# A weight ring laid out by rows, and padding that starts every large matmul operand on a multiple of 64 bytes

## The chip, the cores and the metric

The kernel runs on one core of a Trainium2 chip. The metric is the device time of one execution in microseconds, the median of the runs shown. PE is the matrix engine, PEld its weight loads, DVE the vector engine, ACT the scalar engine, POOL the general engine, SP the queue that issues most transfers (DMAs). SBUF is the on-chip memory from which the engines read; an address below is a byte address within one of its 128 partitions. PSUM takes the results of matmuls.

## The reference, cut to what matters

One block of a hybrid transformer with 2048 tokens of width 1024: normalized and modulated input, a projection to 2832 columns, sliding-window attention beside a bidirectional mLSTM scan, an output projection, and 16 experts that each choose 256 tokens.

```python
hx = modulate(rmsnorm(x, norm1_w), sh1, sc1)
hc = modulate(rmsnorm(ctx, norm1_w), csh1, csc1)
aq, ak, av, mq, mk, mv, mo, gates = jnp.split(h @ w_in, offs, -1)     # for hx and for hc
att = latent_attention(apply_rope(aq), apply_rope(ak), av, cak, cav, sink)
h_sum = bidir_mlstm(mq, mk, mv, li_f, lf_f, li_b, lf_b, st_f, st_b)
x = x + g1 * (concat(att, mlstm_out(h_sum, mo, mlstm_norm_w)) @ w_out)
hx2 = modulate(rmsnorm(x, norm2_w), sh2, sc2)
aff = softmax(hx2 @ w_router); gate, idx = top_k(aff.T, 256)          # per expert
y = (silu(xg @ w_gate) * (xg @ w_up)) @ w_down * gate                 # xg = hx2[idx]
x = x + g2 * zeros.at[idx].add(y)
```

## The kernel before

All large products are kept near fp32 accuracy: each fp32 operand is split into a rounded part (hi, type fp32r) and the rest (lo, fp32r), and three matmuls hi·hi, lo·hi, hi·lo are added up in PSUM. A matmul takes a stationary operand (lhsT, 128 columns, loaded by a LDWEIGHTS) and a moving one (rhs, 256 to 512 columns, streamed). For each operand a partition's row is read from one start address on.

The program has three stages that follow each other.

- **The input stage** (48 to 920 us in the trace). Tokens come in units of 256 (`make_hx` writes hx_hi and hx_lo, 8 tiles of 128 rows by 256 tokens). The 2832 columns of w_in are taken in 22 pieces of 128 columns, in an order of groups (kv, q, mk, mq, mv, mo), four times over, once for each pair of units. `weights` (L717) loads a piece in two halves into w_raw, `split_w` (L745) writes w_hi (ACT, L750) and w_lo (DVE, L756) into a ring of four slots; with the group kv come 16 gate columns, 8 with each of its two pieces, by a small DMA of their own (L739). `tok_chain` (L762) makes outputs with tokens on the partitions: stationary hx, moving a pair of slots (L773), 24 matmuls. `chan_chain` (L779) makes outputs with channels on the partitions: stationary one slot, moving hx (L791). Attention runs in between: scores (L257, L261), transposes of the probabilities (L302), products with the values (L330, L331).
- **The mixing stage** (920 to 1445 us): the mLSTM visits (L1907, L1636) with operands of 258 columns (`vsplit`, `split_state`), and the output projection (`proj`, L1998) with 512 moving columns. Then comes the choice of tokens (to about 1525 us).
- **The expert stage** (1525 to 2093 us): per expert 16 transposes of gathered rows (L2589), 192 matmuls for gate and up (`expert`, L2645; stationary ew, moving xg) and 48 with 512 columns for down (`down`, L2697; stationary h, moving ew).

The order of the instructions is made at build time by a small planner (class Flow): tasks wait for tokens (buffers) and events, each step states the engine and a cost, and the planner always takes the step that can start first, by priority. A cost that is changed, or a wait, shifts the order within a stage. Tiles of one pool stand one behind the other in a partition; a tile starts on a multiple of 32 bytes, and pools on the right side are stacked from the top end.

Of the kernel before, what the change touches and what calls it, by code (L numbers as in the profile page):

```python
# [21 lines left out]
F32 = mybir.dt.float32  # L22
F32R = mybir.dt.float32r
# [332 lines left out]
class Kernel:  # L356
# [18 lines left out]
    def constants(self):  # L375
# [18 lines left out]
        nc.vector.tensor_scalar(self.qw, rows[:, 0:64], -(64 ** -0.5), None, op0=OP.mult)  # L394
        self.nsink = const.tile([128, 8], F32, name="nsink")
        nc.vector.tensor_scalar(self.nsink, self.sink, -1.0, None, op0=OP.mult)
        self.identr = const.tile([128, 128], F32R, name="identr")
# [39 lines left out]
    def phase_in(self):  # L437
        nc, tc = self.nc, self.tc
        with ExitStack() as st:
            pool = lambda name, bufs, **k: st.enter_context(tc.tile_pool(name=name, bufs=bufs, **k))  # L440
            self.ps = pool("psin", 1, space=PSUM)
            self.right, self.mod, self.att = ExitStack(), ExitStack(), ExitStack()
            self.keep = self.outer.enter_context(tc.tile_pool(name="gkeep", bufs=1, side="right"))
            self.hxp = self.right.enter_context(tc.tile_pool(name="hxp", bufs=2, side="right"))
            self.hxs = [self.hx_pair(self.hxp, i) for i in range(2)]
            self.early = ExitStack()
            self.ep = self.early.enter_context(tc.tile_pool(name="early", bufs=1, side="right"))
            self.wp = pool("wring", 1)
            self.w_hi = self.wp.tile([128, 4, KT, 136], F32R, name="w_hi")
            self.w_lo = self.wp.tile([128, 4, KT, 136], F32R, name="w_lo")  # L450
            self.mp = self.mod.enter_context(tc.tile_pool(name="mod", bufs=1))
# [116 lines left out]
    def mod_first(self):  # L568
# [66 lines left out]
        self.pin = self.pool("pin", 2, reuse_waits="tile")  # L635
        self.pa = self.att.enter_context(self.tc.tile_pool(name="att", bufs=2, reuse_waits="tile"))
        self.kt = one.tile([128, 2, 2, NSLOT * 128], F32R, name="kt")
        self.ckt = one.tile([128, 2, 2, 2 * 128], F32R, name="ckt")
# [78 lines left out]
    def weights(self):  # L717
        nc, p, fl, tok = self.nc, self.wp, self.fl, self.tok
        n = 0
        for b in range(4):  # L720
            for name, i in GROUPS:
                c0 = {"kv": 512, "q": 0, "mk": 1280, "mq": 768, "mv": 1792, "mo": 2304}[name] + 256 * i
                for j in range(2):
                    yield tok["slot"]
                    sl = n % 4
                    extra = 2816 + 8 * j if name == "kv" else None
                    w = 128 if extra is None else 136
                    left = [2]
                    if n < 4:
                        yield self.wm_ev[XW_AT[2 + n // 2]]  # L730
                    for k0 in range(0, KT, 4):
                        yield tok["w_raw"]
                        raw = self.buf(p, "w_raw", [128, 4, 136])
                        ks = k0 * 128 * W_COLS
                        yield Q(544)
                        nc.sync.dma_start(raw[:, :, :128], self.dram(self.a["w_in"], ks + c0 + 128 * j,
                                                                     [[W_COLS, 128], [128 * W_COLS, 4], [1, 128]]))
                        if extra is not None:
                            nc.sync.dma_start(raw[:, :, 128:], self.dram(self.a["w_in"], ks + extra,  # L739
                                                                         [[W_COLS, 128], [128 * W_COLS, 4], [1, 8]]))  # L740
                        fl.spawn(self.split_w(raw, sl, k0, w, left, n), PRI["wsp"])
                        fl.issued()
                    n += 1

    def split_w(self, raw, sl, k0, n, left, s):  # L745
        nc, fl = self.nc, self.fl
        for k in range(0, 4, 2):
            hi, lo = (w[:, sl, k0 + k:k0 + k + 2, :n] for w in (self.w_hi, self.w_lo))
            yield A(2 * n)
            nc.scalar.activation(hi, raw[:, k:k + 2, :n], AF.Copy)  # L750
            if WPOOL and k:
                yield G(2 * n)
                nc.gpsimd.tensor_sub(lo, raw[:, k:k + 2, :n], f(hi))
            else:
                yield V(2 * n)
                nc.vector.tensor_sub(lo, raw[:, k:k + 2, :n], f(hi))  # L756
        fl.give(self.tok["w_raw"])
        left[0] -= 1
        if not left[0]:
            fl.fire(self.w_ev[s])  # L760

    def tok_chain(self, sl, unit, t, n):  # L762
        hi, lo, _ = self.hx[unit]
# [3 lines left out]
        for hx, w, evs in ((hi, self.w_hi, self.hh_ev), (lo, self.w_hi, self.hl_ev), (hi, self.w_lo, self.hh_ev)):  # L767
            for k in range(KT):
                if k % CH == 0:
                    for ev in evs[unit][k // 2:(k + CH + 1) // 2]:  # L770
                        yield ev
                    yield "P", CH * (0.108 if n == 128 else 0.114)
                self.nc.tensor.matmul(ps[:, :2 * n].rearrange("p (a b) -> p a b", a=2),  # L773
                                      lhsT=hx[:, k, t * 128:(t + 1) * 128], rhs=w[:, sl:sl + 2, k, :n],
                                      start=(i == 0), stop=(i == 23))
# [3 lines left out]
    def chan_chain(self, sl, units):  # L779
        yield self.tok["mm"]  # L780
        ps = self.buf(self.ps, "mm", [128, 512])
        for j, u in enumerate(units):
            hi, lo, _ = self.hx[u]
            i = 0
            for w, hx, evs in ((self.w_hi, hi, self.hh_ev), (self.w_hi, lo, self.hl_ev), (self.w_lo, hi, self.hh_ev)):
                for k in range(KT):
                    if k % CH == 0:
                        for ev in evs[u][k // 2:(k + CH + 1) // 2]:
                            yield ev
                        yield "P", CH * 0.108  # L790
                    self.nc.tensor.matmul(ps[:, j * 256:(j + 1) * 256], lhsT=w[:, sl, k, 0:128], rhs=hx[:, k, :],  # L791
                                          start=(i == 0), stop=(i == 23))
# [3 lines left out]
    def main(self):  # L796
        fl, tok = self.fl, self.tok
        ctx, n = ("c", 0), 0
        for b in range(4):
            xs = [("x", 2 * b), ("x", 2 * b + 1)]  # L800
            for g in GROUPS:
# [16 lines left out]
                else:  # L818
                    for u in units:
                        yield self.hh_ev[u][0]  # L820
                        for t in range(2):
                            ps = yield from self.tok_chain(sl, u, t, 136 if name == "kv" else 128)
                            if name == "kv":
                                fl.spawn(self.when_open(self.kv_out(ps, u, t)), PRI["kv"])
                            elif name == "q":
# [116 lines left out]
    def head_norm(self, ps, nh, used):  # L942
# [11 lines left out]
        nc.scalar.activation(sq, xr, AF.Square)  # L954
        ss = p.tile([128, nh], F32, name=f"hss{nh}", bufs=3)
        yield V(n)
# [68 lines left out]

    def kv_out(self, ps, u, t):
        nc, p, fl, tok = self.nc, self.pin, self.fl, self.tok
# [13 lines left out]
        def value():  # L1041
            if not ctx and n >= NSLOT:
                yield self.unit_done[n - NSLOT + 1]
            vt = (self.cvt if ctx else self.vt)[:, n if ctx else n % NSLOT]
            pv = ps[:, 136:264].rearrange("p (k d) -> p k d", k=2)
            yield A(128)
# [9 lines left out]
        yield V(16)  # L1056
        pg = ps[:, :272].rearrange("p (a b) -> p a b", a=2)[:, :, 128:136]
        nc.vector.tensor_add(g, pg, self.bg.rearrange("p (a b) -> p a b", a=2))
        used()
        xr = yield from self.head_norm(ps[:, :128], 2, used)  # L1060
        if ctx:
# [522 lines left out]
    def split_state(self, d, C):  # L1584
        nc, p = self.nc, self.pin
        cs = p.tile([128, 4, 258], F32R, name=f"cs{d}", bufs=1)
        for j in range(2):
# [95 lines left out]
    def vsplit(self, vr):  # L1683
        nc = self.nc
        vs = self.buf(self.pin, "vsl", [128, 4, 258], F32R)
        yield from self.copy("v_h", 516, vs[:, :, 0:129], vr)
# [810 lines left out]
    def picks(self):  # L2497
# [4 lines left out]
        self.pg = self.pool("pgather", 2)  # L2502
        p16 = self.p16
        oh = [keep.tile([128, 16, 16], F16, name=f"oh0{i}") for i in range(2)]
        for i in range(2):
# [280 lines left out]
```

## Time and profile before

| what | value |
|---|---|
| median of 3 runs | 2085.2 us (2082.46 to 2087.51) |
| the profiled execution's own time | 2095.2 us |
| its span, first to last instruction | 2093.2 us |
| busy PE, PEld, DVE, ACT, POOL | 90%, 80%, 82%, 59%, 41% |
| mean granted clock of PE | 0.95 |
| instructions of PE | 12921 matmuls |

A matmul's busy time in the profile is longer than the step from one matmul to the next, because they overlap in the engine. How long a stream of equal matmuls takes is read from the start times: the start of one group of x8 to the start of the next, divided by 8. The chain of waits does this too: its pieces do not overlap, so a piece "x168" of 19.61 us has a step of 19.61 / 168 us.

### The profile page before, as it was taken

How to read it: one execution, taken by the hardware profiler on the slowest of the kernel's cores; microseconds unless marked ns; L12 is line 12 of the kernel's file. 1: busy time of each engine (PE TensorE's matmuls, PEld its weight loads, DVE VectorE, ACT ScalarE, POOL GpSimd, SP SyncE). 2: the span in 40 equal slices, each digit the busy share in tenths (PEclk: the TensorE clock that was granted, in tenths of full speed). 3: DMA queues.
4: the chain of work that ended last, by engine and by line, in shares of the span. 5: the costliest groups of instructions: out<-in, count | busy, mean ns of one | idle time of the engine just before them, and what ended most of it. 6: DMA issues, size and time to landing. Idle time of an engine off the chain costs nothing.

```text
span 2093.2 us, 37150 instructions
## 1 busy us (share of the span) xinstructions
PE 1881.3 (90%) x12921; PEld 1677.4 (80%) x12921; DVE 1710.0 (82%) x3846; ACT 1226.6 (59%) x2993; POOL 861.1 (41%) x828
## 2 busy tenths in 40 slices
PE   7799999999999999978888798896299999999997
PEld 3688988898889988966666576685299999999996
DVE  3799679999998799869999999976867777777773
ACT  4477667787777777765555355454254545454541
POOL 0224234423442233225777755421343545444432
PEclk9899999999999999988999899898599999999999
DMA  7343264354432332246666565546358787888782
GB/s 275 96 141 100 71 198 112 118 156 133 116 96 77 96 104 76 80 131 216 213 220 197 180 196 175 165 159 209 128 163 256 223 256 222 256 221 259 220 243 41
DMA packets 291195, 345.14 MB, mean 165 GB/s; under 512 B 27032, under 2 KB 225336, under 8 KB 290112
## 3 DMA queue, kind: packets, MB, share of 16 engines
q1 hardware_dynamic: 280768, 307.64, 47.4%
q0 software_dynamic: 9376, 34.08, 7.0%
q8 instruction: 102, 1.67, 0.3%
q10 hardware_dynamic: 864, 1.05, 0.1%
q14 instruction: 85, 0.70, 0.1%
HBM read 266.50 MB, written 76.09 MB: 164 GB/s over the span
## 4 chain that ended last, share of the span: by engine, by line
PE 54%; DVE 28%; issue 6%; DMA 5%; ACT 5%; POOL 1%; SPq 1%; POOLq 0%; DVEq 0%; ACTq 0%
PE gu L2645 17%; PE mm L773 10%; PE yp L2697 8%; PE po L1998 4%; DVE w_lo L756 3%; DMA w_raw<-in_w_in 2%; PE t L302 2%; PE s L257 1%; PE o L608 1%; PE t L2589 1%; DVE s L279 1%; PE o L331 1%; PE o L330 1%; DVE vsl L1615 1%; ACT w_hi L750 1%
## 5 line engine op out<-in xcount | busy, mean ns | idle before, releaser
L2494 ACT ACTIVATE ew_hi<-ew_raw 128x1024 fp32r<-128x1024 f32 x192 | 202.1, 1056 | 157.7 <-PE yp L2697 91.8
L2454 DVE TENSOR_TENSOR ew_lo<-ew_raw,ew_hi 128x1024 fp32r<-128x1024 f32 x152 | 217.4, 1439 | 33.3 <-issue 17.9
L290 POOL TENSOR_SCALAR P<-P,am 128x640 f32<-128x640 f32 (+1 forms) x128 | 115.0, 899 | 261.9 <-DVE am L288 105.3
L756 DVE TENSOR_TENSOR w_lo<-w_raw,w_hi 128x256 fp32r<-128x256 f32 (+1 forms) x352 | 161.6, 484 | 19.0 <-ACT w_hi L750 17.6
L2717 POOL DMA_INDIRECT out_x<-y,idx x32 | 57.6, 1801 | 271.6 <-DVE y L2711 184.9
L773 PE MATMUL mm<-w_hi,hx_hi 128*128 128x256 f32 (+1 forms) x944 | 144.4, 291 | 5.0 <-DVE moe L933 2.0
L2645 PE MATMUL gu<-xg_hi,ew_hi 128*128 128x256 f32 x1024 | 148.9, 283 | 0.0
L750 ACT ACTIVATE w_hi<-w_raw 128x256 fp32r<-128x256 f32 (+1 forms) x352 | 133.9, 409 | 18.4 <-DMA w_raw<-in_w_in 17.2
L773 PE MATMUL mm<-w_hi,hx_lo 128*128 128x256 f32 (+1 forms) x944 | 142.6, 289 | 0.0
L773 PE MATMUL mm<-w_lo,hx_hi 128*128 128x256 f32 (+1 forms) x944 | 142.6, 287 | 0.0
L2645 PE MATMUL gu<-xg_lo,ew_hi 128*128 128x256 f32 x1024 | 141.7, 280 | 0.0
L2645 PE MATMUL gu<-xg_hi,ew_lo 128*128 128x256 f32 x1024 | 141.4, 280 | 0.0
L773 PEld LDWEIGHTS mm<-w_hi,hx_hi 128*128 128x128 f32 x944 | 125.7, 192 | 8.2 <-DVE moe L933 2.6
L2645 PEld LDWEIGHTS gu<-xg_hi,ew_hi 128*128 128x128 f32 x1024 | 131.8, 189 | 0.1
L2645 PEld LDWEIGHTS gu<-xg_lo,ew_hi 128*128 128x128 f32 x1024 | 129.7, 189 | 0.0
L2645 PEld LDWEIGHTS gu<-xg_hi,ew_lo 128*128 128x128 f32 x1024 | 129.3, 188 | 0.0
L773 PEld LDWEIGHTS mm<-w_hi,hx_lo 128*128 128x128 f32 x944 | 126.0, 192 | 2.9 <-issue 2.1
L773 PEld LDWEIGHTS mm<-w_lo,hx_hi 128*128 128x128 f32 x944 | 125.2, 190 | 2.4 <-issue 1.5
L313 DVE TENSOR_TENSOR pl<-t,ph 128x512 fp32r<-128x512 f32 x156 | 105.6, 683 | 23.6 <-ACT ph L311 22.6
L2711 DVE SCALAR_TENSOR_TENSOR y<-yp,gv,g2b 128x512 f32<-128x512 f32 x64 | 48.0, 751 | 89.9 <-PE yp L2697 89.9
L281 ACT ACTIVATE P<-s,am 128x640 f32<-128x640 f32 (+1 forms) x128 | 99.8, 780 | 29.0 <-DVE am L279 19.5
L311 ACT ACTIVATE ph<-t 128x512 fp32r<-128x512 f32 x156 | 92.0, 594 | 41.9 <-PE t L302 38.3
(483 smaller groups left out, 5731.0 us busy)
## 6 DMA issues: line engine op xcount, KB each, us to landing
w_raw<-in_w_in SPq DMA_DIRECT2D x176, 256.0 KB
ew_raw<-in_w_gate SPq DMA_DIRECT2D x32, 1024.0 KB
ew_raw<-in_w_up SPq DMA_DIRECT2D x32, 1024.0 KB
ew_raw<-in_w_down SPq DMA_DIRECT2D x32, 1024.0 KB
xt<-in_w_mod SPq DMA_DIRECT2D x64, 256.0 KB
out_x<-xl SPq DMA_DIRECT2D x32, 512.0 KB
vraw<-s_mv SPq DMA_DIRECT2D x32, 258.0 KB
raw<-s_mq SPq DMA_DIRECT2D x32, 256.0 KB
```

Of the source, the lines that this page charges most:

```text
L281: nc.scalar.activation(P[:, :n], sc, AF.Exp, bias=m[:, 0:1], scale=-1.0, accum_out=m[:, 1:2])
L290: nc.gpsimd.tensor_scalar(P[:, :n], P[:, :n], m[:, 4:5], 0.0, op0=OP.mult, op1=OP.add)
L311: nc.scalar.activation(hi, pt, AF.Copy)
L313: nc.vector.tensor_sub(lo, pt, f(hi))
L750: nc.scalar.activation(hi, raw[:, k:k + 2, :n], AF.Copy)
L756: nc.vector.tensor_sub(lo, raw[:, k:k + 2, :n], f(hi))
L773: self.nc.tensor.matmul(ps[:, :2 * n].rearrange("p (a b) -> p a b", a=2), lhsT=hx[:, k, t * 128:(t + 1) * 128], rhs=w[:, sl:sl + 2, k, :n] ...
L1998: self.nc.tensor.matmul(po, lhsT=m[:, k, :], rhs=self.wo[k0 + k][wi][:, sl], start=(j == 0), stop=(j == 11))
L2454: (self.nc.vector if eng == "D" else self.nc.gpsimd).tensor_sub(out, x, y)
L2494: nc.scalar.activation(hi[:, sl], raw[:, sl], AF.Copy)
L2645: nc.tensor.matmul(po[:, ft, :], lhsT=w[:, k, ft * 128:(ft + 1) * 128], rhs=x[:, k, :], start=(j == 0), stop=(j == 23))
L2697: nc.tensor.matmul(po[hf], lhsT=hs[i][h][:, ft, t * 128:(t + 1) * 128], rhs=wd[i][w][:, ft, hf * 512:(hf + 1) * 512], start=(j[hf] == 0), ...
```

## The change

It moves no work from one engine to another and leaves the number of matmuls (12702 in the program, some of them taking two rows of the trace) as it is. It has four parts.

1. **Padding.** Tiles of 32 bytes that nobody reads stand in the pools const, gkeep, att and pgather; a small tile has 4 buffers in place of 3; two tiles of 1032 columns are allotted 1040. Everything behind them moves by 32 bytes or a multiple.
2. **The weight ring by rows.** w_hi and w_lo were [4 slots, 8, 136 columns]: a slot's 8 rows lay 544 bytes apart, and a pair of slots was read in two runs 4352 bytes apart. They become [8, 544 columns]: four slots of 128 columns beside each other and 16 columns at either end for the gates. A pair of slots is now one run of 256 columns (272 with the gates).
3. **The gates.** Their 16 columns come with one piece of each kv pair, by one DMA of 16 columns, in place of two DMAs of 8 columns with both pieces. Over the program SP issues 960 DMAs in place of 968.
4. **Costs.** The planner sees 2 x 144 and 2 x 128 columns for the two pieces of kv, in place of twice 2 x 136.

Where the operands start in the two built programs (address modulo 64, moving / stationary):

| line | columns | matmuls | before | after |
|---|---|---|---|---|
| L773 (`tok_chain`) | 256 | 2400 | 0 or 32, two runs / 32 | 0, one run / 0 |
| L773, kv with gates | 272 | 432 | 0 or 32, two runs / 32 | 0, one run / 0 |
| L791 (`chan_chain`) | 256 | 1632 | 32 / 0 or 32 | 0 / 0 |
| L257, L261 scores | 256, 384 | 512 | 32 / 0 | 0 / 0 |
| L330, L331 values | 512 | 312 | 0 / 32 | 0 / 0 |
| L1907, L1636 mLSTM | 258 | 784 | 0, 8, ... 56 / 0 or 32 | 0, 8, 16, 24 / 0 |
| L1998 projection | 512 | 768 | 32 / 32 | 0 / 0 |
| L2645 gate, up | 256 | 3072 | 0 / 32 | 0 / 0 |
| L2697 down | 512 | 768 | 32 / 32 | 0 / 0 |

The transposes read the identity (start 0 before and after) as the moving operand; their stationary operand started at 0 (L302, L1011, L2589) or at 32 (L704, L1601, L1961, L2116) before.

```diff
@@ constants
+        const.tile([128, 8], F32, name="pad")
@@ phase_in
+            self.keep.tile([128, 8], F32, name="padk")
-            self.w_hi = self.wp.tile([128, 4, KT, 136], F32R, name="w_hi")
-            self.w_lo = self.wp.tile([128, 4, KT, 136], F32R, name="w_lo")
+            self.w_hi = self.wp.tile([128, KT, 544], F32R, name="w_hi")
+            self.w_lo = self.wp.tile([128, KT, 544], F32R, name="w_lo")
@@ mod_first
+        self.pa.tile([128, 8], F32, name="pada", bufs=1)
@@ weights
-                    extra = 2816 + 8 * j if name == "kv" else None
-                    w = 128 if extra is None else 136
+                    extra = name == "kv" and j == sl // 2
+                    at = 16 if extra and not j else 0
+                    c1, w = (16 + 128 * sl - at, 144) if extra else (16 + 128 * sl, 128)
...
-                        if extra is not None:
-                            nc.sync.dma_start(raw[:, :, 128:], self.dram(self.a["w_in"], ks + extra,
-                                                                         [[W_COLS, 128], [128 * W_COLS, 4], [1, 8]]))
+                        if extra:
+                            nc.sync.dma_start(raw[:, :, 128 - 8 * at:144 - 8 * at], self.dram(self.a["w_in"], ks + 2816,
+                                                                                            [[W_COLS, 128], [128 * W_COLS, 4], [1, 16]]))
@@ split_w
-            hi, lo = (w[:, sl, k0 + k:k0 + k + 2, :n] for w in (self.w_hi, self.w_lo))
+            hi, lo = (w[:, k0 + k:k0 + k + 2, c:c + n] for w in (self.w_hi, self.w_lo))
@@ tok_chain
-                self.nc.tensor.matmul(ps[:, :2 * n].rearrange("p (a b) -> p a b", a=2),
-                                      lhsT=hx[:, k, t * 128:(t + 1) * 128], rhs=w[:, sl:sl + 2, k, :n],
+                self.nc.tensor.matmul(ps[:, :n], lhsT=hx[:, k, t * 128:(t + 1) * 128], rhs=w[:, k, c:c + n],
                                       start=(i == 0), stop=(i == 23))
@@ chan_chain
-                    self.nc.tensor.matmul(ps[:, j * 256:(j + 1) * 256], lhsT=w[:, sl, k, 0:128], rhs=hx[:, k, :],
+                    self.nc.tensor.matmul(ps[:, j * 256:(j + 1) * 256], lhsT=w[:, k, 16 + 128 * sl:144 + 128 * sl], rhs=hx[:, k, :],
@@ head_norm
-        ss = p.tile([128, nh], F32, name=f"hss{nh}", bufs=3)
+        ss = p.tile([128, nh], F32, name=f"hss{nh}", bufs=4)
@@ split_state (vsplit alike)
-        cs = p.tile([128, 4, 258], F32R, name=f"cs{d}", bufs=1)
+        cs = p.tile([128, 1040], F32R, name=f"cs{d}", bufs=1)[:, 0:1032].rearrange("p (h c) -> p h c", h=4)
@@ picks
+        self.pg.tile([128, 8], F32, name="padg", bufs=1)
```

The instructions of the mixing and expert stages stand in the same order in both programs, on every engine. In the input stage the order differs in many small places. At its beginning SP issues the first weights (w_raw is the buffer that a piece lands in). Before:

```order
L736 DMA w_raw<-in_w_in 128x4x128
L739 DMA w_raw<-in_w_in 128x4x8
L736 DMA w_raw<-in_w_in 128x4x128
L739 DMA w_raw<-in_w_in 128x4x8
L736 DMA w_raw<-in_w_in 128x4x128
L739 DMA w_raw<-in_w_in 128x4x8
L736 DMA w_raw<-in_w_in 128x4x128
L739 DMA w_raw<-in_w_in 128x4x8
L736 DMA w_raw<-in_w_in 128x4x128 x2
```

And after:

```order
L740 DMA w_raw<-in_w_in 128x4x128
L743 DMA w_raw<-in_w_in 128x4x16
L740 DMA w_raw<-in_w_in 128x4x128
L743 DMA w_raw<-in_w_in 128x4x16
L740 DMA w_raw<-in_w_in 128x4x128 x6
```

The fourth large load has two small ones ahead of it in place of three, and the small one behind it is gone. On PE the first chain (mm is its PSUM tile, xe the second unit's raw tokens, which are transposed) begins after these transposes before:

```order
L618 MATMUL mm<-cst,row_242 128x8 x4
L704 MATMUL t<-cst,xe_192 128x128
L704 MATMUL t<-cst,xe_203 128x128
...
L704 MATMUL tr<-cst,xe_192 128x128
L704 MATMUL tr<-cst,xe_203 128x128
L773 MATMUL mm<-w_hi,hx_hi_94 128x272 x8
```

and ahead of them after:

```order
L620 MATMUL mm<-cst,row_243 128x8 x4
L777 MATMUL mm<-w_hi,hx_hi_96 128x272 x8
L777 MATMUL mm<-w_hi,hx_lo_97 128x272 x8
L777 MATMUL mm<-w_lo,hx_hi_96 128x272 x8
L707 MATMUL t<-cst,xe_194 128x128
L707 MATMUL t<-cst,xe_205 128x128
```

So 24 matmuls of the first chain now stand ahead of twelve transposes of the second unit.

## Rows read from the trace of the kernel before

**Rows 1.** The page's busy time by engine, its slices for PE, DVE, the granted clock and DMA, and the shares of the chain that ended last.

```profile
PE 1881.3 (90%) x12921; PEld 1677.4 (80%) x12921; DVE 1710.0 (82%) x3846; ACT 1226.6 (59%) x2993; POOL 861.1 (41%) x828
...
PEclk9899999999999999988999899898599999999999
...
PE 54%; DVE 28%; issue 6%; DMA 5%; ACT 5%; POOL 1%; SPq 1%; POOLq 0%; DVEq 0%; ACTq 0%
PE gu L2645 17%; PE mm L773 10%; PE yp L2697 8%; PE po L1998 4%; DVE w_lo L756 3%; DMA w_raw<-in_w_in 2%; PE t L302 2%; PE s L257 1%; PE o L608 1%; PE t L2589 1%; DVE s L279 1%; PE o L331 1%; PE o L330 1%; DVE vsl L1615 1%; ACT w_hi L750 1%
```

**Rows 2.** Busy time of each engine by stage. Columns: from and to, length, busy PE, PEld, DVE, ACT, POOL with counts, granted clock, DMA share, GB/s.

```profile
48.00:920.00 872.00, 823.59 (x6271) 772.31 (x6270) 757.20 (x2112) 635.26 (x1732) 301.41 (x434) 0.98 0.38 108
920.00:1445.00 525.00, 444.04 (x2345) 350.90 (x2345) 472.15 (x1052) 275.37 (x803) 284.82 (x237) 0.91 0.60 192
1525.00:2093.00 568.00, 555.82 (x4039) 524.38 (x4037) 404.64 (x383) 275.29 (x366) 247.75 (x137) 0.99 0.75 217
```

**Rows 3.** The chain that ended last within 0 to 920 us, within 920 to 1445 us and within 1525 to 2093 us, shares by line.

```profile
by line: PE mm L773 21.8%; DVE w_lo L756 6.4%; issue 5.9%; DMA w_raw<-in_w_in 5.7%; PE t L302 4.2%; PE s L257 3.3%; PE o L608 3.2%; DVE s L279 2.9%; PE o L331 2.6%; PE o L330 2.5%; ACT w_hi L750 2.3%; PE s L261 1.9%; ACT P L281 1.9%; DVE cv
by line: PE po L1998 16.0%; issue 8.2%; DVE vsl L1615 4.2%; PE h L1907 3.8%; PE t L2125 3.6%; DVE ho L1936 3.3%; DVE C L1615 3.2%; DVE hh L1894 3.1%; DVE decb L1720 3.0%; DVE rr L1917 2.9%; DVE vsl L1610 2.8%; DVE tmp L1615 2.7%; PE h L1636
by line: PE gu L2645 62.7%; PE yp L2697 29.8%; PE t L2589 4.4%; DMA out_x<-y,idx 1.1%; POOLq L2782 0.3%; issue 0.1%; DVE y L2711 0.1%; POOLq L2717 0.0%
```

**Rows 4.** One expert's pieces of that chain, and the start of the next one. Columns: start in us, us, what.

```profile
1560.36 19.61 PE gu L2645 x168
1579.97 10.90 PE yp L2697 x48
1590.87 0.87 PE t L2589 x8
```

**Rows 5.** The timeline of PE in an expert's gate and up part. Columns: start, us of the merged row, engine, line, what it reads and writes, count.

```profile
1704.06 1.10 PE L2645 MATMUL gu<-xg_lo,ew_hi 128*128 128x256 f32 x8
...
1720.08 0.63 PE L2645 MATMUL gu<-xg_hi,ew_hi 128*128 128x256 f32 x4
```

**Rows 6.** The timeline of PE at 224 us: a product with values (both of its moving operands start at a multiple of 64) and, behind it, transposes whose weights start at one too.

```profile
223.69 0.39 PE L330 MATMUL o<-ph,vt 128*128 128x512 f32 x1
223.92 0.39 PE L331 MATMUL o<-pl,vt 128*128 128x512 f32 x1
224.16 0.60 PE L302 MATMUL t<-cst,P 128*128 128x128 f32 x4
```

**Rows 7.** The timeline of PE at 970 us: the projection, then one mLSTM visit, 16 matmuls whose moving operands start at all multiples of 8 and whose weights start at 0 or 32 (wh and wl at 0, qh and ql at 32).

```profile
969.89 1.10 PE L1998 MATMUL po<-wo_lo,mixh 128*128 128x512 f32 x4
970.83 0.28 PE L1907 MATMUL h<-vsl,wh 128*128 128x258 f32 x1
970.95 0.28 PE L1907 MATMUL h<-vsl,wl 128*128 128x258 f32 x1
971.07 0.29 PE L1907 MATMUL h<-cs,qh 128*128 128x258 f32 x1
971.19 0.28 PE L1907 MATMUL h<-cs,ql 128*128 128x258 f32 x1
971.31 0.28 PE L1907 MATMUL h<-vsl,wh 128*128 128x258 f32 x1
...
972.75 0.63 PE L1998 MATMUL po<-wo_hi,mixh 128*128 128x512 f32 x2
```

**Rows 8.** The timeline of PE in a chain of `tok_chain` (moving operand in two runs), in one of `chan_chain` (one run), and the first and last full group of a chain with the gates; the ten groups from 704.23 to 714.29 us follow each other without a gap.

```profile
301.01 1.12 PE L773 MATMUL mm<-w_lo,hx_hi 128*128 128x256 f32 x8
...
304.82 0.40 PE L773 MATMUL mm<-w_hi,hx_hi 128*128 128x256 f32 x2
...
527.86 1.13 PE L791 MATMUL mm<-hx_hi,w_hi 128*128 128x256 f32 x8
528.82 1.10 PE L791 MATMUL mm<-hx_lo,w_hi 128*128 128x256 f32 x8
529.76 0.64 PE L791 MATMUL mm<-hx_hi,w_lo 128*128 128x256 f32 x4
...
704.23 1.16 PE L773 MATMUL mm<-w_hi,hx_hi 128*128 128x272 f32 x8
...
714.29 1.17 PE L773 MATMUL mm<-w_hi,hx_lo 128*128 128x272 f32 x8
```

**Rows 9.** The timeline of SP's issues before the first chain, and the piece of the chain of waits that ends just ahead of it.

```profile
28.98 2.50 SPq L736 DMA_DIRECT2D w_raw<-in_w_in  x1
31.52 0.59 SPq L739 DMA_DIRECT2D w_raw<-in_w_in  x1
35.44 0.37 SPq L736 DMA_DIRECT2D w_raw<-in_w_in  x1
35.85 0.51 SPq L739 DMA_DIRECT2D w_raw<-in_w_in  x1
39.94 4.70 DMA w_raw<-in_w_in
47.83 5.35 PE mm L773 x40
```

More of the change, by code (lines that the diff above doesn't have):

```diff
@@ L732, in weights, with split_w @@
                         yield tok["w_raw"]
-                        raw = self.buf(p, "w_raw", [128, 4, 136])
+                        raw = self.buf(p, "w_raw", [128, 4, 144])
                         ks = k0 * 128 * W_COLS
                         yield Q(544)
-                        nc.sync.dma_start(raw[:, :, :128], self.dram(self.a["w_in"], ks + c0 + 128 * j,
+                        nc.sync.dma_start(raw[:, :, at:at + 128], self.dram(self.a["w_in"], ks + c0 + 128 * j,
                                                                      [[W_COLS, 128], [128 * W_COLS, 4], [1, 128]]))
-                        if extra is not None:
-                            nc.sync.dma_start(raw[:, :, 128:], self.dram(self.a["w_in"], ks + extra,
-                                                                         [[W_COLS, 128], [128 * W_COLS, 4], [1, 8]]))
-                        fl.spawn(self.split_w(raw, sl, k0, w, left, n), PRI["wsp"])
+                        if extra:
+                            nc.sync.dma_start(raw[:, :, 128 - 8 * at:144 - 8 * at], self.dram(self.a["w_in"], ks + 2816,
+                                                                                            [[W_COLS, 128], [128 * W_COLS, 4], [1, 16]]))
+                        fl.spawn(self.split_w(raw, c1, k0, w, left, n), PRI["wsp"])
                         fl.issued()
                     n += 1
-    def split_w(self, raw, sl, k0, n, left, s):
+    def split_w(self, raw, c, k0, n, left, s):
         nc, fl = self.nc, self.fl
         for k in range(0, 4, 2):
-            hi, lo = (w[:, sl, k0 + k:k0 + k + 2, :n] for w in (self.w_hi, self.w_lo))
+            hi, lo = (w[:, k0 + k:k0 + k + 2, c:c + n] for w in (self.w_hi, self.w_lo))
             yield A(2 * n)
@@ L760, in split_w, with tok_chain @@
             fl.fire(self.w_ev[s])
-    def tok_chain(self, sl, unit, t, n):
+    def tok_chain(self, c, unit, t, n):
         hi, lo, _ = self.hx[unit]
@@ L771, in tok_chain @@
                         yield ev
-                    yield "P", CH * (0.108 if n == 128 else 0.114)
-                self.nc.tensor.matmul(ps[:, :2 * n].rearrange("p (a b) -> p a b", a=2),
-                                      lhsT=hx[:, k, t * 128:(t + 1) * 128], rhs=w[:, sl:sl + 2, k, :n],
+                    yield "P", CH * (0.108 if n == 256 else 0.114)
+                self.nc.tensor.matmul(ps[:, :n], lhsT=hx[:, k, t * 128:(t + 1) * 128], rhs=w[:, k, c:c + n],
                                       start=(i == 0), stop=(i == 23))
@@ L821, in main @@
                         for t in range(2):
-                            ps = yield from self.tok_chain(sl, u, t, 136 if name == "kv" else 128)
+                            at = 16 if name == "kv" and not sl else 0
+                            ps = yield from self.tok_chain(16 + 128 * sl - at, u, t, 272 if name == "kv" else 256)
                             if name == "kv":
-                                fl.spawn(self.when_open(self.kv_out(ps, u, t)), PRI["kv"])
+                                fl.spawn(self.when_open(self.kv_out(ps, u, t, at)), PRI["kv"])
                             elif name == "q":
@@ L1024, in q_out, with kv_out @@
         fl.fire(self.q_ev[n, i])
-    def kv_out(self, ps, u, t):
+    def kv_out(self, ps, u, t, at):
         nc, p, fl, tok = self.nc, self.pin, self.fl, self.tok
@@ L1044, in value @@
             vt = (self.cvt if ctx else self.vt)[:, n if ctx else n % NSLOT]
-            pv = ps[:, 136:264].rearrange("p (k d) -> p k d", k=2)
+            pv = ps[:, at + 128:at + 256].rearrange("p (k d) -> p k d", k=2)
             yield A(128)
@@ L1056, in kv_out @@
         yield V(16)
-        pg = ps[:, :272].rearrange("p (a b) -> p a b", a=2)[:, :, 128:136]
+        pg = ps[:, 256 - 16 * at:272 - 16 * at].rearrange("p (a b) -> p a b", a=2)
         nc.vector.tensor_add(g, pg, self.bg.rearrange("p (a b) -> p a b", a=2))
         used()
-        xr = yield from self.head_norm(ps[:, :128], 2, used)
+        xr = yield from self.head_norm(ps[:, at:at + 128], 2, used)
         if ctx:
@@ L1684, in vsplit @@
         nc = self.nc
-        vs = self.buf(self.pin, "vsl", [128, 4, 258], F32R)
+        vs = self.buf(self.pin, "vsl", [128, 1040], F32R)[:, 0:1032].rearrange("p (h c) -> p h c", h=4)
         yield from self.copy("v_h", 516, vs[:, :, 0:129], vr)
```

## The prediction, written before the run

> **What bounds the kernel now.** I read the page first. [rows 1] PE is busy 1881.3 us of the span, DVE 1710.0, and the chain that ended last is 54% PE and 28% DVE; its largest single piece is `gu` of L2645, then `mm` of L773 and `yp` of L2697. [...]
>
> Next the busy time by stage [rows 2], because a share over the whole span mixes stages. In the input stage PE is busy 824 of 872 us with DVE at 757 beside it; in the mixing stage DVE (472 of 525) is ahead of PE (444); in the expert stage PE is busy 556 of 568 and no other engine passes 405. So a nanosecond saved on an expert matmul comes out at the end whole, one saved in the input stage in part, one saved in the mixing stage mostly where the projection runs.
>
> The chain by stage gives the same with weights [rows 3]: `gu` and `yp` are 62.7% and 29.8% of the 568 us of the expert stage (356 and 169 us), `mm` of L773 is 21.8% of the first 920 us (201 us), `po` of L1998 16.0% of the mixing stage (84 us). This is why the sum below is one of steps per matmul.
>
> **The steps, and what alignment does to them in this trace.** All times a matmul needs from its start to the next, at a granted clock near full:
>
> - L2645, 256 columns, moving at 0 and stationary at 32: the chain has 19.61 / 168 = 116.7 ns [rows 4]; in the timeline 17 groups of eight lie between 1704.06 and 1720.08 us, 16.02 / 136 = 117.8 [rows 5]. I use the second, which is without the merging of the chain's pieces.
> - L2697, 512 columns, both at 32: 10.90 / 48 = 227.1 ns [rows 4].
> - L2589, a transpose of 128 columns, both operands at 0 already: 0.87 / 8 = 108.8 ns [rows 4].
> - L330 and L331, 512 columns, moving at 0: 0.47 us for two, 235 ns. The second of them loads, while it streams, the weights of a transpose that also start at 0, and it isn't quicker (240, its fellow 230) [rows 6].
> - L1907, 258 columns: 120 ns each, with moving operands that start at eight different residues and weights at 0 or 32. L1998 with 512 columns, both at 32: 0.94 / 4 = 235 ns [rows 7].
> - L773 in two runs: 3.81 / 32 = 119.1 ns; with 272 columns 10.06 / 80 = 125.8 ns. L791 in one run, moving at 32: 117.5 ns in its second group of eight (0.94 / 8), and 118.8 over both [rows 8].
>
> [...] What the trace lacks is a stream of 256 or 512 columns in which the moving operand, its own weights and the next weights all start at 0. That gap is where I may be wrong.
>
> [...]
>
> **The change part by part.**
>
> Alignment of operands on PE: 0. The bounds are the nearest rows. [...] Upwards, gate and up become as slow as L773's 119.1, and down as slow as 235: 3072 x 1.3 = 4.0 and 768 x 7.9 = 6.1 us. Between ends so far apart I take the value of the rows whose residues differ and whose steps don't.
>
> The moving pair of slots in one run in place of two: L773 comes to L791's step, 119.1 - 117.5 = 1.6 ns, over 2832 matmuls 4.5 us of PE. L773 takes in all 2400 x 119.1 + 432 x 125.8 ns = 340 us, of which 201 are on the chain, six tenths; so -2.7 us. Bounds 0 (the 1.6 ns are something else: L791's first group had 120) and -4.5.
>
> The gates' DMAs: SP issues a small one in 0.5 to 0.6 us, and before the first chain the fourth large load has one less ahead of it [rows 9]. That chain starts right behind such a load (4.70 us on the chain), so -0.5; the other small DMAs lie beside PE work. The twelve transposes that now stand behind the first 24 matmuls are still needed before the second unit, so they only change places: they ran while weights were awaited, and if nothing else fills that time it costs 12 times L2589's 108.8 ns, 1.3 us; I take 0.
>
> [...] The split of a kv pair writes 144 + 128 columns in place of twice 136, the same sum on ACT and DVE: 0.
>
> The planner's new order in the input stage: it neither adds nor removes instructions, but each place where PE meets a load late or early is worth one such wait, 4.70 us; I take 0, bounds two of them either way, 9 us. In the mixing and expert stages the order stands.
>
> Sum: 0 - 2.7 - 0.5 - 1 + 0 = -4.2 us against the profiled execution's own 2095.2 (span 2093.2 and 2.0 around it), 2091.0. That execution is 10.0 us above the median of the runs, 2085.2; the difference is carried over whole, and the forecast is 2081.0.
>
> **The rivals.**
>
> *Forecast (chance 0.53): alignment is not what the steps wait for.* 2081.0, its own range 2070 to 2090 by the reordering and the bounds of the small terms. [...]
>
> *The starts are what they wait for (0.33).* [...] With the small terms (1.5) -73.5 against 2095.2, so 2021.7, and 2011.7 as a median; own range 1985 to 2040. For it: the missing row, and the rows that contradict it have two columns more (258 is no multiple of 64 bytes) or 512 columns. Against it: [rows 6], where the stream and the next weights start at 0 and 240 ns are paid, and DVE with 757 us of 872, which would leave less than six tenths.
>
> [...]
>
> *Equal starts collide, slower (0.14).* PE reads the moving operand and the next weights at the same time. In L2645 they now begin 32 bytes apart and would then begin on the same residue; if two reads that begin alike get in each other's way, L2645 goes to 119.1, L2697 to the 235 of L1998 (whose operands start alike, at 32), and L773 keeps 119.1 in spite of the single run: +4.0 + 6.1 - 0.5 = +9.6, so 2094.8. It decides from 4.2 us on, under half its price. [...]
>
> That the program doesn't do what is said is excluded by the starts in the built programs.
>
> **How the numbers follow.** 0.2% or 4.2 us is about what a measurement of this kernel can tell from no change: faster is below 2081.0, slower above 2089.4. The forecast lies on the first of these edges, so its 0.53 splits into 0.27 faster, 0.19 same, 0.07 slower. The second rival's 0.33 is all faster. The third's 0.14 is 0.01 same and 0.13 slower. Together 0.60, 0.20, 0.20. The range of 8 in 10 must take in the rival of 2011.7 and most of the third: 2004 leaves out a third of the second rival (0.11), 2094 somewhat over half of the third (0.08). The forecast's own range beside it is 2070 to 2090.
>
> **What would show it.** The step of L2645, over a stretch as long as [rows 5], says most: 117 to 118 ns for the forecast, 109 to 111 for the second rival, 119 and more for the third. L2697: 227 per step, or about 216, or 235. L773 should have L791's step, whatever that is. The input stage should be 2 to 5 us shorter with the same instructions, the mixing stage unchanged to a few us. I am wrong if the expert stage is no longer 568 us within 3, and wrong only about the order if the steps stay but the input stage moves by over 9 us.

## The result and the profile after

The changed kernel takes 2104.48 us (median of 6 runs, 2101.26 to 2106.78), the kernel before 2086.36 beside it (6 runs): ratio 1.0084, 95% interval 1.0065 to 1.0103. It is 18 us slower, and outside the range that was given.

The profiled execution of the changed kernel took 2101.26 us, 3 us under its median; that of before took 2095.2, some 9 us over its own. The two profiles therefore show only 6 of the 18 us. For the search for the loss the profile of the first experiment below is the better partner (2088.36 us): it has all of the change but the order of before, and lies 13 us under that of after. The page of after, against [rows 1]:

```profile
PE 1876.4 (89%) x12921; PEld 1670.2 (80%) x12921; DVE 1711.5 (82%) x3846; ACT 1227.9 (58%) x2993; POOL 869.2 (41%) x828
...
PEclk9799999999999999988999899998599999999999
...
PE 56%; DVE 29%; issue 6%; DMA 4%; ACT 4%; SPq 0%; POOL 0%; POOLq 0%; DVEq 0%; ACTq 0%
```

No engine has much more to do: PE is busy 5 us less, POOL 8 us more with the same 828 instructions. The granted clock is lower in one slice, the second digit, 7 in place of 8: that is 52 to 105 us.

The steps of the expert stage come first, since the second and third rival stood or fell with them. The chain of waits in one expert, against [rows 4]:

```profile
1565.03 19.79 PE gu L2650 x168
1584.82 10.91 PE yp L2702 x48
1595.73 0.87 PE t L2594 x8
```

19.79 / 168 = 117.8 ns and 10.91 / 48 = 227.3 ns, with every operand on a multiple of 64. Neither 109 nor 119, neither 216 nor 235: the stage that holds a quarter of the time hardly notices the change.

Where the time went is seen in the windows of the input stage's beginning. First after, then the first experiment. Columns as in [rows 2].

```profile
48.00:70.00 22.00, 18.34 (x106) 17.08 (x107) 14.70 (x58) 11.95 (x40) 3.12 (x7) 0.72 0.24 72
70.00:100.00 30.00, 16.06 (x81) 12.52 (x80) 13.66 (x45) 9.67 (x30) 7.55 (x9) 0.66 0.11 33
100.00:130.00 30.00, 27.49 (x232) 26.27 (x231) 28.22 (x86) 17.25 (x57) 8.93 (x17) 1.00 0.56 166
```

```profile
48.00:70.00 22.00, 17.52 (x112) 15.65 (x112) 16.41 (x57) 13.10 (x41) 6.58 (x10) 0.85 0.10 28
70.00:100.00 30.00, 22.76 (x165) 20.41 (x164) 22.49 (x78) 13.53 (x47) 7.09 (x11) 0.82 0.49 146
100.00:130.00 30.00, 27.86 (x223) 25.67 (x224) 28.40 (x78) 18.94 (x54) 12.19 (x23) 1.00 0.36 99
```

Between 70 and 100 us PE issues 81 matmuls in place of 165, at a granted clock of 0.66 in place of 0.82. From 100 us on the two are alike. The first chain of `chan_chain` (L791 before, L794 after) is a good milestone: it begins at 98.1 us before, at 97.6 in experiment 1 and at 111.9 us after. That is 13.8 or 14.3 us, lost within the first 112 us. From there on nothing is lost against experiment 1, as the first expert's long piece in the chain of waits shows, first after, then experiment 1:

```profile
1530.22 19.32 PE gu L2650 x164
```

```profile
1516.94 19.32 PE gu L2651 x164
```

There after lies 13.3 us behind, and at the end of the span 13.0 (2099.5 against 2086.5).

PE's timeline from 73 us on, where the time is lost, in the kernel after:

```profile
73.68 0.77 PE L777 MATMUL mm<-w_hi,hx_hi 128*128 128x272 f32 x4
78.62 1.09 PE L707 MATMUL tr<-cst,xt 128*128 128x128 f32 x4 [4.18 <-DVE gatet L1097]
80.93 0.45 PE L1075 MATMUL tr<-cst,hxr 128*128 128x128 f32 x1 [1.22 <-ACT hxv L676]
...
85.09 0.44 PE L1075 MATMUL tr<-cst,hxr 128*128 128x128 f32 x1 [2.98 <-DVE gatet L1097]
...
89.25 1.09 PE L707 MATMUL tr<-cst,xt 128*128 128x128 f32 x4 [2.98 <-DVE gatet L1097]
89.99 0.80 PE L777 MATMUL mm<-w_hi,hx_hi 128*128 128x272 f32 x2
91.97 0.82 PE L777 MATMUL mm<-w_hi,hx_hi 128*128 128x272 f32 x2 [1.18 <-DVE hx_hi L684]
```

All of these transposes write `tr`, a PSUM tile of which there is one. Those of L1075 to L1077 belong to the outputs of kv (keys and gates), those of L707 turn the context's tokens, and the next chain on PE needs the turned context. The order puts three kv outputs (at 73.0, 80.9 and 85.1 us) ahead of the context's last two groups of four transposes (78.6 and 89.3). Each has to pass through the one `tr`, and a pass takes 4 us: 80.93 to 85.09, 85.09 to 89.25. The one from 73.0 to 78.6 takes 5.6, since other work of DVE stands between its copies. The chain of waits over one of them:

```profile
81.59 0.54 PE tr L1077 x2
...
82.15 0.27 ACT kt L1087
82.42 0.01 issue
82.44 0.27 ACT kt L1089
82.70 0.01 issue
82.72 0.27 ACT kt L1087
82.99 0.01 issue
83.00 0.28 ACT kt L1089
...
84.53 0.42 DVE gatet L1097
84.96 0.14 issue
85.09 0.44 PE tr L1075
```

Four copies on ACT, four subtractions and one copy on DVE, then `tr` is free. The next chain stands behind these passes on PE and begins at 89.99 us. In this stretch the granted clock is low, 0.50 from 80 to 90 us, and what PE does get to do takes longer: eight matmuls of L777 have 2.02 us at 94.40 (granted clock 0.50 from 94 to 97 us) and 1.16 at 98.89 (1.00 from 98.5 to 101 us).

### The profile page after: what moved, and what is told of

Read it like the earlier page. It is cut to its first block, busy times and chain, and to the rows that moved or that the text cites. A ratio compares the mean times of both kernels' runs of the same rounds, so it can differ in the third digit from the quotient of the medians.

```text
span 2099.5 us, 37138 instructions
## 1 busy us (share of the span) xinstructions
PE 1876.4 (89%) x12921; PEld 1670.2 (80%) x12921; DVE 1711.5 (82%) x3846; ACT 1227.9 (58%) x2993; POOL 869.2 (41%) x828
## 4 chain that ended last, share of the span: by engine, by line
PE 56%; DVE 29%; issue 6%; DMA 4%; ACT 4%; SPq 0%; POOL 0%; POOLq 0%; DVEq 0%; ACTq 0%
PE gu L2650 17%; PE mm L777 11%; PE yp L2702 8%; PE po L2002 3%; DVE w_lo L760 3%; PE t L302 3%; PE mm L794 2%; PE s L257 2%; PE o L610 1%; PE o L331 1%; PE o L330 1%; PE t L2594 1%; DVE vsl L1619 1%; DVE s L279 1%; DMA w_raw<-in_w_in 1%
## 5 line engine op out<-in xcount | busy, mean ns | idle before, releaser
L777 PE MATMUL mm<-w_hi,hx_hi 128*128 128x256 f32 (+1 forms) x944 | 146.1, 292 | 13.8 <-ACT hx_hi L681 5.1
L777 PE MATMUL mm<-w_hi,hx_lo 128*128 128x256 f32 (+1 forms) x944 | 142.1, 289 | 0.5 <-DVE hx_lo L688 0.5
L777 PEld LDWEIGHTS mm<-w_hi,hx_hi 128*128 128x128 f32 x944 | 126.5, 193 | 19.3 <-ACT hx_hi L681 5.2
L777 PE MATMUL mm<-w_lo,hx_hi 128*128 128x256 f32 (+1 forms) x944 | 141.3, 288 | 0.0
L777 PEld LDWEIGHTS mm<-w_lo,hx_hi 128*128 128x128 f32 x944 | 125.2, 192 | 2.2 <-issue 1.5
L777 PEld LDWEIGHTS mm<-w_hi,hx_lo 128*128 128x128 f32 x944 | 125.3, 193 | 1.9 <-DVE hx_lo L688 0.9
```

Source lines behind the costliest of these rows:

```text
L777: self.nc.tensor.matmul(ps[:, :n], lhsT=hx[:, k, t * 128:(t + 1) * 128], rhs=w[:, k, c:c + n], start=(i == 0), stop=(i == 23))
```

## The experiments

"Order of before" means that on every engine the instructions stand as in the kernel before (on SP, but for the small DMAs of the gates). Ratios are to the kernel before on the same chip, with their 95% interval.

**1. The change without its costs.** The planner is told 136 columns for both pieces of kv:

```diff
-            yield A(2 * n)
+            m = 136 if s % 22 < 2 else n
+            yield A(2 * m)
```

(and the same where w_lo is written). This gives the order of before, with the new starts, ring and DMAs.

> The whole change (padding, ring by rows, gates by one DMA) but the planner is told 2 x 136 columns for both pieces of kv, as before; with that, every engine has the order of before. Theory 'order' (the new costs, by the order they make, are the loss): as fast as before, 2086 us within 4, or faster by the up to 4 us of the small terms; L1097's waits at 70 to 95 us are gone. Theory 'starts' (the equal or new start addresses slow the engines): as slow as the changed kernel, 2104 us within 4. Theory 'gates' (one DMA of 16 columns per pair, or pieces of 144 and 128 columns, come late): 2104 us too.

2087.22 us, ratio 1.0007 (0.9997 to 1.0017): no difference. Parts 1 to 3 of the change are worth nothing that can be measured, and the loss sits in part 4.

**2. The costs alone**, in the kernel before:

```diff
-            yield A(2 * n)
+            m = n if n == 128 else 144 if s % 2 == s % 4 // 2 else 128
+            yield A(2 * m)
```

> The kernel before, where only the planner's costs for the pieces of kv are those of the change (2 x 144 and 2 x 128); order of the changed kernel, with the old addresses, ring and DMAs. Theory 'order': 2104 us within 5, with the PE idle stretch between 70 and 95 us. Theory 'starts' and theory 'gates': 2086 us within 4.

2104.03 us, ratio 1.0080 (1.0064 to 1.0096). Two numbers that the planner reads make the whole loss; the edit touches nothing else, and PE, ACT, DVE and POOL then have the order of the changed kernel.

**3. The change without padding** (the four tiles, the fourth small buffer and the 1040 columns taken out; order of after).

> The changed kernel without the tiles of padding and the 1040-column allotments: operands start at 32 modulo 64 again wherever padding had moved them, the order is that of the changed kernel. Theory 'order': 2104 us within 5, steps of gate and up 117 to 119 ns as in both kernels. Theory 'starts': 2086 us within 4. Theory 'gates': 2104 us.

2101.85 us, ratio 1.0087 (1.0070 to 1.0103), as the changed kernel. This and the first run exclude the starts as the cause, from both sides.

**4 and 5. Which of the costs.** The changed kernel with the new costs for the first two pieces only, and for all but the first two:

```diff
-            yield A(2 * n)
+            m = 136 if s % 22 < 2 and s > 1 else n
+            yield A(2 * m)
```

```diff
-            yield A(2 * n)
+            m = 136 if s < 2 else n
+            yield A(2 * m)
```

> The changed kernel, where the planner is told 144 and 128 columns for the first two pieces of kv only, and 2 x 136 for the later six, as before. Theory 'start-up' (all the loss arises before 100 us, from the place of the first chain, ahead of the second unit's transposes, and of the kv transposes, ahead of the context's): 2101 to 2105 us, with the lag behind the old order of 13 us or more at 100 us. Theory 'spread' (each of the four passes gives away a few us, 18 / 4 each): about 2090 us.

> The reverse: 2 x 136 columns told for the first two pieces, 144 and 128 for the later six; the order up to about 150 us is that of before. Theory 'start-up': 2086 us within 4. Theory 'spread': about 2099 us.

2102.58 us, ratio 1.0075 (1.0060 to 1.0091), and 2090.12 us, ratio 1.0014 (1.0004 to 1.0024). Nearly all comes from the first two pieces; about 3 us come from the later passes (the 2090.12 is just beyond the 4 us that theory 'start-up' allowed).

**6 and 7. The context first.** The kv transposes of the first two units wait in the planner until the context's are placed, in the changed kernel (6) and in the kernel before (7):

```diff
+            elif k2 == 3 and u == ("c", 0):
+                fl.fire(self.c_turned)
...
         yield ev
+        if not ctx and n < 4:
+            yield self.c_turned
         yield tok["tr"]
```

> The changed kernel, where the transposes of the first four kv tiles wait in the planner until the context's four groups of transposes have been placed on PE (they share one PSUM buffer, tr). Theory 'tr' (three trips of some 4 us through the single tr buffer, with nothing else for PE, are the 10 us lost between 80 and 100 us): 2094 us or less, 10 us of 18 back, and PE's wait for gatet gone from 75 to 92 us. Rival 'clock' (the loss is the low granted clock after the start, wherever it comes from; the tr trips only sit in it): 2100 us or more.

> The same rule put into the kernel before, whose PE waits 5 us for one such trip at 69 to 74 us. Theory 'tr': 2081 us within 3, about one trip of 5 us less. Rival: what PE waits for there is the context's rows (rs_t), not the buffer, and the time stays at 2086 within 3.

6: 2090.6 us, ratio 1.0015 (1.0002 to 1.0028), 14 us less than the changed kernel. 7: 2081.93 us, ratio 0.9969 (0.9958 to 0.9981), faster than both kernels: before had one such pass too. PE waited 5.2 us there; first PE, then DVE in the kernel before:

```profile
73.87 1.09 PE L704 MATMUL tr<-cst,xt 128*128 128x128 f32 x4 [5.19 <-DVE rs_t L551]
```

```profile
73.31 0.41 DVE L1093 COPY gatet<-tr 8x256 f32<-8x256 f32 x1
73.65 0.15 DVE L551 TENSOR_SCALAR rs_t<-rs_t 128x2 f32<-128x2 f32 x1
```

The profile puts the wait down to rs_t of L551, an operation that stands on DVE right behind the copy that empties `tr` (L1093). PE goes on 0.15 us after the end of that copy, and 0.14 after L1097 in the changed kernel (78.48 to 78.62 us). With the rule the wait is gone, so it was the one for `tr`:

```profile
70.37 1.12 PE L704 MATMUL tr<-cst,xt 128*128 128x128 f32 x4 [0.36 <-ACT hxv L673]
```

The low clock of the stretch goes as well (in 6 the granted clock from 70 to 100 us is 0.94), and with 2090.6 us the rival that needed 2100 or more falls.

But the 14 us are not 14 of the 18. The rule gives the old costs 6 us too, so experiment 6 is to be compared with 7 and 10, which have the rule and the old costs: it is still 10 us slower (1.0015 against 0.9969 and 0.9967). Roughly, since each ratio has its interval of 2 to 4 us, the passes through `tr` are 8 of the 18 us, and 10 us have another place.

**8 and 9. The second unit's transposes first.** In the changed kernel the first chain waits in the planner for three of the second unit's four groups of transposes (8); the same with the context first (9).

```diff
+            if k2 == 2 and u == ("x", 1):
+                fl.fire(self.x_turned)
...
         ctx, n = ("c", 0), 0
+        yield self.x_turned
```

> The changed kernel, where the first chain waits in the planner until three of the second unit's four groups of transposes have been placed on PE, as they stand in the order before; the kv transposes still stand ahead of the context's. Theory: the first 5 us of the lag (at 60 us) come from the chain placed ahead of transposes that could have run while PE waited, so 2097 to 2101 us, about 4 to 5 us less than the changed kernel, and the 10 us at 80 to 100 us stay. Rival: the start only shifts the wait, and the time stays at 2103 within 3.

> The changed kernel with both rules, the context's transposes ahead of the kv transposes and the second unit's ahead of the first chain. Theory (the two places are the whole loss): 2081 to 2087 us, as the kernel before or as that with the first rule. Rival (further places of the new order cost as much): 2090 us as with the first rule alone.

8: 2101.72 us, ratio 1.0065 (1.0049 to 1.0081); 9: 2086.28 us, ratio 0.9989 (0.9980 to 0.9998), as its theory said. The time of 8 does not tell theory and rival apart: the median is in the rival's range (2100 to 2106), the ratio is the theory's 4 us under that of the changed kernel. The trace does, and the theory's reason was wrong. PE's timeline in 8:

```profile
48.41 1.76 PE L707 MATMUL t<-cst,xe 128*128 128x128 f32 x7 [5.66 <-DVE xe L534]
```

The transposes could not have run earlier: their input is late. L534 on DVE scales the second unit's two tiles of rows. In the kernel after:

```profile
39.41 0.46 DVE L760 TENSOR_TENSOR w_lo<-w_raw,w_hi 128x288 fp32r<-128x288 f32 x1 [3.82 <-ACT w_hi L754]
...
40.77 0.74 DVE L534 TENSOR_SCALAR xe<-xe,xrs 128x1024 f32<-128x1024 f32 x1
...
47.33 1.28 DVE L688 TENSOR_TENSOR hx_lo<-xv,hx_hi 128x512 fp32r<-128x512 f32 x2
48.53 0.74 DVE L534 TENSOR_SCALAR xe<-xe,xrs 128x1024 f32<-128x1024 f32 x1
```

and in experiment 1, with the order of before:

```profile
36.31 0.75 DVE L534 TENSOR_SCALAR xe<-xe,xrs 128x1024 f32<-128x1024 f32 x1
...
39.84 0.46 DVE L761 TENSOR_TENSOR w_lo<-w_raw,w_hi 128x288 fp32r<-128x288 f32 x1 [2.78 <-ACT w_hi L755]
...
41.38 0.75 DVE L534 TENSOR_SCALAR xe<-xe,xrs 128x1024 f32<-128x1024 f32 x1
```

With the new costs both L534 stand behind other work, though the first one's factors were ready at 35.5 us (L555) and DVE then sat idle for 3.82 us. The second stands behind the first unit's hx_lo and ends 7 us later. What looked like an order of PE was a place on DVE. What 8 won it may have won at `tr`: there two kv outputs stand ahead of the context's last transposes, in the changed kernel four.

**10. The old costs with the context first**: all of the change but its costs, and the rule of 6 and 7.

> The whole change with the old costs told to the planner and the context's transposes ahead of the kv transposes: the order of the run of before with that rule (2081.9 us), at the new start addresses, with the ring by rows and the new DMAs for the gates. Theory (starts, ring and DMAs are worth nothing that can be measured): 2082 us within 3. Rival (my forecast's small terms, 2 to 4 us, or a loss by the starts): 2078 to 2080, or 2086 and more.

2081.88 us, ratio 0.9967 (0.9955 to 0.9979), against 0.9969 for experiment 7 with the same order at the old starts. That is the cleanest comparison of the starts, the ring and the DMAs: no difference, with intervals of 2.5 us to either side (the two medians, 0.05 us apart, are from different chips, and that they agree so closely is luck).

**11 and 12. The rows first.** One priority in the changed kernel, for the norm of the second unit's rows (11), and the same with the context first (12):

```diff
-                self.fl.spawn(self.norm_x(x, xs[t][1]), PRI["norm"])
+                self.fl.spawn(self.norm_x(x, xs[t][1]), -1 if u == ("x", 1) else PRI["norm"])
```

> The changed kernel, where the norm of the second unit's rows (L534 on xe) goes first in the planner; on DVE its second half then stands ahead of the weight splits and of the first unit's hx_lo, as it does before, and PE gets the second unit's transposes ahead of the first chain and one kv tile only ahead of the context's last transposes. Theory 'late rows' (the L534 that the new costs place 7 us later is the root of both places): 2086 us within 4, the PE wait for xe and the tr trips gone. Rival (the late rows are worth only the first 4 us of the lag, and the tr trips come back by another way): 2094 us or more.

> The same with the context's transposes ahead of the kv transposes too: the whole change with both places mended. Theory: 2082 us within 3, as the old order with the context first. Rival (the order of the later passes, which keeps the new costs, loses some us of its own, as the 2090 with new costs in the later passes alone could say): 2085 to 2088 us.

11: 2088.73 us, ratio 1.0006 (0.9994 to 1.0018). DVE's L534 there:

```profile
34.81 0.75 DVE L534 TENSOR_SCALAR xe<-xe,xrs 128x1024 f32<-128x1024 f32 x1
...
40.01 0.75 DVE L534 TENSOR_SCALAR xe<-xe,xrs 128x1024 f32<-128x1024 f32 x1
```

With the rows back in their place the planner puts only one kv output ahead of the context's last transposes again, and the loss is gone, with the new costs kept everywhere. Late rows and passes through `tr` thus have one root, the place of the second unit's norm, which ends with L534. The link between them stands on SP: in the program `load_x` places the loads of the next unit's rows, here the context's, only when both L534 of the unit before are placed. In the kernel after they go out behind eight large weight loads, in experiment 1 behind six (two more stand ahead of the rows shown):

```profile
28.63 18.23 SPq L740 DMA_DIRECT2D w_raw<-in_w_in  x6
46.91 1.80 SPq L514 DMA_DIRECT2D xt<-in_ctx  x2
```

```profile
29.59 12.01 SPq L740 DMA_DIRECT2D w_raw<-in_w_in  x4
41.64 0.98 SPq L514 DMA_DIRECT2D xt<-in_ctx  x2
```

In all runs whose second L534 starts late (47.6 to 50.8 us: after, 2, 3, 4, 6, 8 and 9) the context's loads start at 46.0 to 50.2 us, in all others (L534 at 40.0 to 42.3) at 40.4 to 42.5. So the context's transposes come later, and kv outputs get ahead of them. Experiment 11 moves both back at once: it shows the root, not what the second unit's rows and the context's rows cost each. Why 144 and 128 columns make the planner place L534 later was not followed.

12: 2085.40 us, ratio 0.9996 (0.9985 to 1.0008), where the rival was nearer: the 6 us that remain against experiments 7 and 10 could be the later passes, to which experiment 5 gives 3 us (1.0014, up to 1.0024), but no run shows the place.

The milestone of all runs goes with the times:

| run | first `chan_chain` starts at, us | ratio |
|---|---|---|
| before | 98.1 | 1 |
| after | 111.9 | 1.0084 |
| 1, old costs | 97.6 | 1.0007 |
| 2, costs alone | 114.4 | 1.0080 |
| 3, no padding | 111.2 | 1.0087 |
| 4, first costs | 110.6 | 1.0075 |
| 5, later costs | 100.3 | 1.0014 |
| 6, context first | 98.3 | 1.0015 |
| 7, before, context first | 95.0 | 0.9969 |
| 8, transposes first | 102.8 | 1.0065 |
| 9, both rules | 93.9 | 0.9989 |
| 10, old costs, context first | 91.6 | 0.9967 |
| 11, rows first | 97.1 | 1.0006 |
| 12, rows and context first | 88.7 | 0.9996 |

It is not proportional: in 8 and 12, and a little in 9, part of what is won by then is given back later. In 8 the same matmul that stands 5 us behind experiment 1 at 100 us stands 11 us behind at 200.

## Why the prediction was wrong

**Alignment of operands, taken at 0: right.** The forecast's mechanism held. The mean step of L2645 over the expert stage is 117.9 ns in the four kernels with the old starts (before, 2, 3, 7) and 118.6 in those with the new ones (after, 1, 10), L2697's 227.2 against 227.3, L773's 124.0 before against 123.0 after (without the stretches of low clock, steps over 400 ns left out), L791's 120.3 against 119.5. That is +2.2 us (3072 x 0.7 ns) in the expert stage and, starts and ring together, some -4 us of PE (2832 x 1.0 and 1632 x 0.8 ns) in the input stage, of which six tenths would reach the end: nothing, by the sum and by experiments 1 and 10.

**The second rival fell** by its own test: the missing row now exists, both operands and the next weights on multiples of 64, and the step is 117.8 ns, not 109. No run shows the -73.5 us of its sum, from which its 2011.7 and with it the range's lower end come, nor the 216 ns of its test for L2697: at the new starts L2697 takes 227.3, and experiments 1 and 10 show no gain (1.0007, and 0.9967 against 0.9969 at the old starts).

**Two readings under the rivals' prices were wrong.** The 116.7 of [rows 4] and the 117.8 of [rows 5] are not one step with and without the chain's merging but two experts with different steps: the chain of before gives the expert of [rows 5] 19.79 / 168 = 117.8 as well:

```profile
1700.92 19.79 PE gu L2645 x168
```

And the second rival's 109 for L2645 is the 108.8 ns of the transposes, which have 128 columns. From 256 columns to 512 the step grows from 117.8 [rows 5] to 227.1 ns [rows 4], 0.43 ns per column. Estimated from that, 128 columns are 55 ns, so the transposes' 108.8 are not their columns alone, and were no bound for a 256-column step.

**The third rival had the sign of the result and not its reason.** Gate and up did become slower, by 0.7 ns where it had 1.3, but the projection of down stayed at 227 and the sum was 2 us where it needed 10.

**One run in place of two, -2.7, the gates' DMAs, -0.5, and the starts for DMAs, ACT and DVE, -1: too large.** L773 gained 1.0 ns per step where 1.6 were taken, by starts and ring together, and did not come to L791's step (122.0 with 256 columns, against 119.5). No run shows the -1 by itself; experiment 1 leaves at most 0.6 us of gain for all three (its interval begins at 0.9997).

**The step that failed is the planner's new order, "I take 0, bounds two of them either way, 9 us".** It measured 17 us by experiment 2's ratio, 18.5 by its medians. The prediction's own sign for this case, steps that stay and an input stage that moves by over 9 us, came true. Both the value and the bound were wrong, for three reasons that its own text shows:

- It priced a moved instruction by a wait of PE for a load, 4.7 us. What moved was L534 on DVE, a step of 0.7 us with a whole unit behind it, and with it the loads of the context's rows, 5.3 us later on SP. The listing ahead of the prediction shows the eight large weight loads in place of six; what follows them wasn't asked.
- It had the very place in its rows, twelve transposes of the second unit now behind the first chain, and said that they only change places. It didn't ask what they had waited for. That they now stand later was a sign that their input is late, and the order on the input's engine, DVE, was never compared, though DVE is 757 of 872 us busy in that stage.
- It took a reshuffle as symmetric. Experiments 6 and 7 show one place where it is not: a single buffer (`tr`) that two kinds of work share. Which of them goes first decides whether three passes of 4 us lie beside a chain on PE or ahead of it.

The stage by stage reading was right in itself, and helped to overlook this: the mean of 872 us says nothing of the first 60, in which PE waits for DVE and for `tr`.

## What to carry to other kernels

A change of a planner's costs is a change of the program, and is to be read as one: compare the order on every engine, not only on the one that the argument is about, and for each group that moved look up who releases it. Look first at the start of a stage and at buffers of which there is one. And an edit that is meant to move data can be tried without its effect on the order, by telling the planner the old numbers; here that run alone separated the two. A rule that mends the changed kernel is to be tried in the kernel before as well: what it gives there is no part of the loss.

The best version is the order of before with the context's transposes ahead of the kv transposes (experiments 7 and 10, 0.3% faster than before); with that, the padding and the ring by rows cost and bring nothing.

## What the runs showed beside it

With the old starts, two experts of three ran gate and up at 116.7 ns per step and every third at 117.8, over the whole stage; with all starts on multiples of 64 all sixteen ran their long pieces at 117.8. Experiment 3, without the padding but with the ring by rows, has the old pattern, so it goes with the padding. The chain of experiment 7 and then of experiment 10:

```profile
1622.90 19.61 PE gu L2651 x168
1657.97 19.61 PE gu L2651 x168
1693.09 19.79 PE gu L2651 x168
```

```profile
1617.62 19.79 PE gu L2657 x168
1652.90 19.79 PE gu L2657 x168
1688.18 19.79 PE gu L2657 x168
```

Yet the three is not in the operands' start addresses: xg has two buffers and ew's four serve six tiles per expert, so both repeat after two experts. The buffers of gathered rows, three for two tiles per expert, do repeat after three; no run follows this up. What gives the 1.1 ns back in two experts of three was not tried.
